# A hybrid decoder layer on one core: 26 of 96 input projections in a stage of their own, 22 of them in pairs with seven block products

## The chip, the core and the metric

The kernel runs on one core of one Trainium2 chip. A core has a matrix engine (PE, TensorE), which reads its two operands from the on-chip memory SBUF and writes to the accumulators in PSUM; three engines for elementwise work (DVE or VectorE, ACT or ScalarE, POOL or GpSimd); and DMA queues, which here are all issued by SP (SyncE), in order. Each engine works through its own list of instructions in a fixed order and waits on semaphores where it needs what another engine makes. The metric is device microseconds of one execution; lower is better.

## The reference, cut to what matters

One layer of a decoder, for a prompt of 1024 tokens and for eight samples of 8 tokens, with the same weights. The kernel treats them as one matrix of TT = 1088 tokens, with the channels on the partitions.

```
h = rmsnorm(x) * (1 + scale) + shift             # scale, shift, gate from a conditioning vector
q, k, v, g_att, z, xBC, dt, g_a, g_b = split(h @ w_in)
att  = 3 groups of dilated windowed attention (prompt; sample over a cache), combined by softmax weights
xBC  = silu(causal_conv4(xBC)); dt = softplus(dt + bias)
y    = chunked_scan(x, dt, B, C, state) + d_skip * x        # Mamba-2 (SSD), chunks of 128
y    = group_rmsnorm(y * silu(z))
out  = sigmoid(g_a) * ((att * silu(g_att)) @ w_att) + sigmoid(g_b) * (y @ w_ssm)
return rmsnorm(x + gate * (out @ w_out)), new caches, new states
```

All sizes are float32, D = 1024. The columns of w_in make 96 tiles of 128 columns (and a narrow one for dt): 12 each of q, k and v (three groups by four pairs of heads), 4 of the attention gate, 16 of z, 24 of x, B and C, 16 of the merge gates.

## The kernel before

Each matrix product of float32 numbers is made of three products of rounded numbers: a value is split into a high part, rounded to the format the matrix engine takes (`fp32r`), and the remainder, and hi x hi, lo x hi and hi x lo are added up in PSUM (`mm3`, lines 193 to 198). So one of the 96 projections is 8 (tiles along the inner dimension) x 3 (terms) x 3 (chunks of 368, 368 and 352 tokens) = 72 matmuls, each with its own load of a 128x128 weight tile. The tiles `h_hi`, `h_lo` of the modulated input stay in SBUF; a weight tile is loaded (`load_w`, `wraw`), split by ACT (`whi`) and DVE (`wlo`), and fetched one projection ahead (`fetch`).

The program has a front (rmsnorm and modulation, with two projections run "early", k by k, as the input tiles come), an attention stage, an SSD stage and an output stage. In the two stages in the middle the order of PE is written out by a recording layer. `run` (line 259) goes through a list of projections, `jobs`. Beside it runs a generator, the side work: `attention` or `side`, which yields how long (in the layer's own count of time) the next step should wait, or after which projection it may come. Every few matmuls of a projection the layer asks whether the side step is due (`Order.poll`) and if so puts the step's matmuls in between. A job that needs a side step to be done first (its marks, for a buffer) makes the layer write out side steps until it is, due or not (`Order.until`). So the order is fixed when the program is built: how much projection work lies between two side steps is what covers the time that DVE, ACT, POOL and DMA need between them.

Side work of the attention stage, for each pair of heads: three prompt groups (scores `s`, softmax on DVE and ACT, transposes `pt`, values `o`), and then the sample block: scores against the cached keys (`sA`, `sB`, with four key tiles `kt` at a time, and `sC`), the softmax of `sm`, its transposes `spt`, the products `so` with seven cached value tiles `vt`, and `soT` to turn the result. `kt`, `vt` and the combination weights `wb` share five buffers (tag `kv`).

Side work of the SSD stage, in four quarters: B and C of a quarter are turned and multiplied (`tt`, `cb`), and then four x tiles, each with `tt` (turn x), `stt` (chunk states), `yo` (carried state), `sts` (state of the samples) and `yd` (diagonal part, with the decay table `csb`). The table is loaded per tile (line 973) into one buffer, which `yd` reads last; DVE subtracts, ACT takes the exponential, DVE multiplies (lines 977 to 985). `sts` and `yd` use two PSUM banks in turn (`bankA`), and DVE frees them (lines 1072 and 1089). At the quarter's end `ms` sums squares by 18 one-column matmuls.

Of the kernel before, what the change touches and what calls it, by code (L numbers as in the profile page):

```python
# [9 lines left out]
F32 = mybir.dt.float32  # L10
# [20 lines left out]
CHUNKS = ((0, 368), (368, 368), (736, 352))  # L31
EPS = 1e-6
# [24 lines left out]
class Order:  # L57
# [47 lines left out]
    def finish(self):  # L105
        self.until(None)
# [3 lines left out]
def trunk(ctx: ExitStack, tc: tile.TileContext, I, O):  # L110
# [64 lines left out]
    wp = hctx.enter_context(pool("wp", 2, side="right"))  # L175
# [49 lines left out]
    def passes():  # L225

        for ks in (range(i, i + 2) for i in range(0, KO, 2)):
            for k in ks:
                yield k, 0, 0
                yield k, 1, 0  # L230
            for k in ks:
                yield k, 0, 1

    def project_early(js, banks):

        ws = [load_w(w_in(j), KO, 128, wp)[:2] for j in js]
        ps = [[b[i](f"early{n}") for i in range(3)] for n, b in enumerate(banks)]
        for k, a, b in passes():
            for w, p in zip(ws, ps):
                for (c0, cn), q in zip(CHUNKS, p):  # L240
                    PE.matmul(q[:, :cn], w[a][:, k, :], (h_hi, h_lo)[b][k][:, c0:c0 + cn], start=(k, a, b) == (0, 0, 0),
                              stop=(k, a, b) == (KO - 1, 0, 1))
# [44 lines left out]
    def w_in(j):  # L287
        return I["w_in"][j]


    with pool("ph0", 2) as p0:
        xT = [p0.tile([128, TT], F32, name=f"xT{k}", bufs=1) for k in range(KO)]
# [13 lines left out]
        def ada(q):  # L306
# [13 lines left out]
            fs = slice(2 * q, 2 * q + 2)  # L320
# [49 lines left out]
        for q in range(4):  # L370
            ada(q)
            for f in (2 * q, 2 * q + 1):
                modulate(f)
        project_early((J_K, J_Q), ([bankPJ] * 3, [bankA, bankA, bankC]))


# [73 lines left out]
    gates = list(range(16))  # L450
# [36 lines left out]
    region = ctx.enter_context(ExitStack())  # L487
    region.enter_context(tc.manual_schedule(engines={mybir.EngineType.PE}))
    with ExitStack() as actx:
# [31 lines left out]
        def attention_jobs(hp, g):  # L521
# [8 lines left out]
            def masks():  # L530
# [3 lines left out]

            yield (("k", n), J_K + g * 4 + hp, (("s", n - 2),) if n > 1 else (),
                   tile_of("k", 2, lambda t, c0, cn, ps: evac_to(t, g, c0, cn, ps)),
                   lambda: store_kv(0, g, hp, tiles[n, "k"]))
            yield (("q", n), J_Q + g * 4 + hp, (("s", n - 2),) if n > 1 else (),
                   tile_of("q", 2, lambda t, c0, cn, ps: evac_to(t, g, c0, cn, ps, 0.125)), masks)
# [287 lines left out]
    with ExitStack() as bctx:  # L827
# [17 lines left out]
        def conv_job(name, j, marks, late, dst):  # L845
# [52 lines left out]
        def jobs():  # L898
            for gr in range(4):
# [389 lines left out]
def _arrays(i):  # L1289
# [18 lines left out]
    for n in ("dt_bias", "a_log"):  # L1308
# [8 lines left out]
        "w_ada": w_ada[:, :2 * D].reshape(8, 128, 2, 4, 256).transpose(3, 0, 1, 2, 4).reshape(4, 8, 128, 512), "w_gate": w_ada[:, 2 * D:].reshape(8, 128, D), "b_gate": i["b_ada"][0][2 * D:],  # L1317
# [52 lines left out]
```

## Time and profile before

| | |
|---|---|
| median of 3 runs | 1938.38 us (1936.6 to 1940.47) |
| profiled execution, its own time | 1937.77 us |
| its span, first to last instruction | 1935.9 us |
| PE busy | 1873.6 us (97%), 13065 matmuls |
| PE weight loads busy | 1760.3 us (91%) |
| DVE / ACT / POOL busy | 1062.1 / 644.9 / 327.7 us |
| DMA | 269.54 MB, mean 139 GB/s |
| granted PE clock, mean | 0.993 |

How to read it: matmuls are pipelined, and a row's duration is that of one matmul from start to modelled end, so durations overlap; what one costs in a stream is the distance between starts. A float32 matmul that isn't split is two records. The "idle" behind a row is the time before it in which the engine had nothing to run, with what ended it. Front to about 69 us, attention to 777, SSD to 1545, then the output stage.

### The profile page before, as it was taken

Reading aid. Unit: us, or ns where it says so; the run is one execution under the profiler, and the core shown is the slowest. Engines: PE = TensorE matmul, PEld = TensorE weight load, DVE = VectorE, ACT = ScalarE, POOL = GpSimd, SP = SyncE. Lnnn points to the kernel's source line nnn. Section 1 sums busy time; section 2 is a strip of 40 time slices with the busy share of each in tenths; the row PEclk is TensorE's granted clock in tenths of the full one; section 3 lists DMA queues with packets and bytes.
Section 4 is the critical chain, followed back from the end, with each engine's and each line's share of the span. In section 5 each row is a group of like instructions: output and inputs, shape, how many; then the busy total and the mean of one; then the engine's idle time right before and its main releaser. Section 6 shows DMA issues by size and latency. Waiting matters only on the chain.

```text
span 1935.9 us, 31991 instructions
## 1 busy us (share of the span) xinstructions
PE 1873.6 (97%) x13065; PEld 1760.3 (91%) x13065; DVE 1062.1 (55%) x1974; ACT 644.9 (33%) x1260; POOL 327.7 (17%) x356
## 2 busy tenths in 40 slices
PE   5999999999999999999999999999999999999998
PEld 4989989988998998999999999999999899999987
DVE  5643243324324323577757775767679655466654
ACT  4443324313423432424342335233533331131222
POOL 2200010001002001132314221422142300000400
PEclk9999999999999999999999999999999999999999
DMA  8322462273256227434443543344233453364322
GB/s 338 121 69 102 132 223 69 87 221 132 96 156 195 83 89 238 148 124 164 148 136 114 169 159 124 117 155 138 81 99 121 153 188 117 127 200 148 123 87 76
DMA packets 108986, 269.54 MB, mean 139 GB/s; under 512 B 41600, under 2 KB 50632, under 8 KB 105576
## 3 DMA queue, kind: packets, MB, share of 16 engines
q1 hardware_dynamic: 108840, 267.51, 42.1%
q8 instruction: 102, 1.67, 0.4%
q14 instruction: 44, 0.36, 0.1%
HBM read 224.93 MB, written 80.26 MB: 158 GB/s over the span
## 4 chain that ended last, share of the span: by engine, by line
PE 50%; DVE 7%; DMA 6%; issue 3%; ACT 2%; POOL 0%; SPq 0%; ACTq 0%; DVEq 0%; POOLq 0%
PE pj L196 12%; PE pj L197 12%; PE pj L198 12%; DMA csb<-cs_d 3%; PE yd L205 2%; PE fo L1207 2%; PE fo L1205 2%; PE fo L1206 2%; PE yo L205 1%; DMA yx<-u_d 1%; DVE wlo L190 1%; DVE csb L977 1%; DVE csb L985 1%; PE sts L205 1%; PE stt L205 1%
## 5 line engine op out<-in xcount | busy, mean ns | idle before, releaser
L196 PE MATMUL pj<-h_hi,whi 128*128 128x368 f32 x2256 | 757.1, 336 | 5.2 <-DVE zs L892 4.7
L198 PE MATMUL pj<-h_lo,whi 128*128 128x368 f32 x2256 | 740.6, 328 | 0.0
L197 PE MATMUL pj<-h_hi,wlo 128*128 128x368 f32 x2256 | 740.1, 328 | 0.0
L196 PEld LDWEIGHTS pj<-h_hi,whi 128*128 128x128 f32 x2256 | 426.1, 189 | 30.9 <-issue 21.1
L197 PEld LDWEIGHTS pj<-h_hi,wlo 128*128 128x128 f32 x2256 | 426.3, 189 | 0.7
L198 PEld LDWEIGHTS pj<-h_lo,whi 128*128 128x128 f32 x2256 | 425.9, 189 | 0.0
L190 DVE TENSOR_TENSOR wlo<-wraw,whi 128x1024 fp32r<-128x1024 f32 (+1 forms) x136 | 163.5, 1202 | 247.8 <-ACT whi L189 245.5
L189 ACT ACTIVATE whi<-wraw 128x1024 fp32r<-128x1024 f32 (+1 forms) x136 | 126.6, 931 | 377.3 <-PE pj L198 369.9
L196 PE MATMUL pj<-yhi,whi 128*128 128x368 f32 (+1 forms) x480 | 157.5, 328 | 1.2 <-DVE acc L1169 1.1
L197 PE MATMUL pj<-yhi,wlo 128*128 128x368 f32 (+1 forms) x480 | 157.7, 328 | 0.2
L198 PE MATMUL pj<-ylo,whi 128*128 128x368 f32 (+1 forms) x480 | 157.1, 327 | 0.0
L626 ACT ACTIVATE pr<-pr,st 128x128 f32<-128x128 f32 (+1 forms) x192 | 83.9, 438 | 88.9 <-DVE st L623 88.7
L197 PEld LDWEIGHTS pj<-yhi,wlo 128*128 128x128 f32 x480 | 90.1, 188 | 3.0 <-issue 2.1
L196 PEld LDWEIGHTS pj<-yhi,whi 128*128 128x128 f32 x480 | 90.1, 188 | 3.0 <-ACT whi L189 1.4
L198 PEld LDWEIGHTS pj<-ylo,whi 128*128 128x128 f32 x480 | 90.1, 188 | 0.0
L875 DVE SCALAR_TENSOR_TENSOR xc<-raw,cw,xc 128x1112 f32<-128x1112 f32 x60 | 82.2, 1369 | 3.1 <-ACT xc L873 2.2
L645 DVE COPY pT<-pt 128x512 f32<-128x512 f32 x40 | 27.6, 689 | 102.3 <-ACT pT L647 40.4
L977 DVE TENSOR_TENSOR csb<-tok,csb 128x2048 f32<-128x2048 f32 x16 | 45.2, 2824 | 45.9 <-DMA csb<-cs_d 45.9
L1174 POOL TENSOR_TENSOR acc<-acc,ta 128x368 f32<-128x368 f32 (+1 forms) x24 | 24.2, 1010 | 263.8 <-DVE ta L1173 263.8
L506 DVE COPY k<-pj 128x368 f32<-128x368 f32 (+2 forms) x44 | 24.0, 581 | 81.3 <-PE pj L198 79.8
L858 ACT ACTIVATE raw<-pj 128x368 f32<-128x368 f32 (+1 forms) x72 | 31.9, 446 | 87.2 <-PE pj L198 84.5
L623 DVE CUSTOM_DVE_ANT_0 pr<-s,msk 128x128 f32<-128x128 f32 (+1 forms) x192 | 55.4, 346 | 7.8 <-PE s L205 7.5
(282 smaller groups left out, 2533.5 us busy)
## 6 DMA issues: line engine op xcount, KB each, us to landing
wraw<-in_w_in SPq DMA_DIRECT2D x96, 512.0 KB, 3.9
csb<-cs_d SPq DMA_DIRECT2D x16, 1088.0 KB, 6.5
kt<-in_kc SPq DMA_DIRECT2D x32, 448.0 KB, 4.6
out_kc<-in_kc SPq DMA_DIRECT2D x32, 448.0 KB, 4.7
out_vc<-in_vc SPq DMA_DIRECT2D x28, 512.0 KB, 5.1
vt<-in_vc SPq DMA_DIRECT2D x28, 512.0 KB, 5.9
sg_d<-sg SPq DMA_DIRECT2D x16, 544.0 KB, 3.0
ecs<-cs_d SPq DMA_DIRECT2D x32, 272.0 KB, 5.0
```

The lines of the kernel that those rows point to most:

```text
L189: S.activation(hi, raw, AF.Copy)
L190: V.tensor_sub(lo, raw, hi.bitcast(F32))
L196: PE.matmul(ps, whi[:, k, :], xhi[k], start=first and k == 0, stop=False)
L197: PE.matmul(ps, wlo[:, k, :], xhi[k], start=False, stop=False)
L198: PE.matmul(ps, whi[:, k, :], xlo[k], start=False, stop=last and k == n - 1)
L205: PE.matmul(out, w, x, **kw)
L623: V.tensor_tensor_reduce(out=pr[:, h, c0:c0 + m], in0=ps[h][:, c0:c0 + m], in1=msk[:, h, w - m:w], scale=-1.0, scalar=3e38, op0=OP.add, op ...
L626: S.activation(pr[:, h, c0:c0 + m], pr[:, h, c0:c0 + m], AF.Exp, scale=-1.0, bias=st[:, 0, h, u:u + 1], accum_out=st[:, 1, h, u:u + 1])
L875: V.scalar_tensor_tensor(c, raw[:, t:t + CONV], cw[:, j, t:t + 1], c, op0=OP.mult, op1=OP.add)
L977: V.tensor_tensor(csb[:, :, :T].rearrange("p h (c l) -> p h c l", l=CH), tok[:, :8, 32 + h0:34 + h0].rearrange("p c h -> p h c")[:, :, :, ...
L1205: PE.matmul(ps, hi, whi[:, k, cs], start=k == 0, stop=False)
L1206: PE.matmul(ps, lo, whi[:, k, cs], start=False, stop=False)
```

## The change

A stage of its own stands between the front and the attention stage. It makes 26 projections: all 12 of q, the 8 even ones of z, and 6 of the 16 merge gates. Two of the gates are the early ones now (k and q were before), and two more are made whole, as before, at the two ends of the stage (`whole`). The other 22 go in 11 pairs. For a pair, the two 128-column weight tiles and the input are taken as 2x2 blocks (output tile by inner half; inner half by half of the tokens), and Strassen's scheme in Winograd's form makes the four result blocks from seven block products instead of eight. Each product has 4 inner tiles x 3 terms, for two halves of 272 columns: 7 x 2 x 12 = 168 matmuls of 272 columns, where two plain projections have 144 of 368 and 352. The combinations of input blocks (T1 to T4) are made once, the weight combinations (`factors`) for every pair, one pair ahead. Results go to DRAM (`q_d`, `z_d`, `sg_d`) and q and z are read back when the stages need them; the lists of jobs of the two stages lose these projections. The side work and its waits (the yields) are unchanged. In the front, `modulate` takes an input tile with its partner four tiles on, and keeps the modulated input in float32 for the combinations.

```diff
+    def project_early(js, banks, pool_, raws):
 ...
-            fs = slice(2 * q, 2 * q + 2)
+            fs = slice(q, KO, KH)
 ...
-            S.activation(h_hi[f][:, :T], h[:, :T], AF.Identity, bias=shift)
-            S.activation(h_hi[f][:, T:], h[:, T:], AF.Copy)
-            V.scalar_tensor_tensor(h_lo[f][:, :T], h[:, :T], shift, h_hi[f][:, :T].bitcast(F32), op0=OP.add, op1=OP.subtract)
-            G.tensor_tensor(h_lo[f][:, T:], h[:, T:], h_hi[f][:, T:].bitcast(F32), op=OP.subtract)
+            S.activation(h[:, :T], h[:, :T], AF.Identity, bias=shift)
+            S.activation(h_hi[f], h, AF.Copy)
+            V.tensor_sub(h_lo[f], h, h_hi[f].bitcast(F32))
 ...
-        project_early((J_K, J_Q), ([bankPJ] * 3, [bankA, bankA, bankC]))
+        project_early((J_GA, J_GA + 1), ([bankPJ] * 3, [bankA, bankA, bankC]), we, rawp)
 ...
+    for k in (0, 3, 1, 2):
+        n = k + KH
+        b11, b12, b21, b22 = xT[k][:, L], xT[k][:, R], xT[n][:, L], xT[n][:, R]
+        t = [tp.tile([128, 2, TH], F32R, name=f"t{k}{i}") for i in range(4)]
+        V.tensor_sub(b11, b12, b11)
+        G.tensor_tensor(b12, b22, b12, op=OP.subtract)
+        V.tensor_sub(b22, b22, b11)
+        V.tensor_sub(b21, b21, b22)
+        for x, r in zip(t, (b11, b22, b12, b21)):
+            S.activation(x[:, 0], r, AF.Copy)
+            V.tensor_sub(x[:, 1], r, x[:, 0].bitcast(F32))
 ...
+    whole(2, [(hi[:, k, :], lo[:, k, :]) for k in range(KO)], bankPJ, we.tile([128, TT], F32, tag="y", name="sg", bufs=1))
 ...
+        def factors(j0, j1):
+            (a11, a12), (a21, a22) = load_raw(j0), load_raw(j1)
 ...
+            G.tensor_tensor(s1, a21, a22, op=OP.add)
+            def parts(src):
+                op = ring.tile([128, 2, KH, 128], F32R, tag="op", name="op")
+                S.activation(op[:, 0], src, AF.Copy)
+                V.tensor_sub(op[:, 1], src, op[:, 0].bitcast(F32))
+                return op
+            yield parts(a11)
+            V.tensor_sub(s2, s1, a11)
+            yield parts(s2)
 ...
+        def product(ps, op, b, c0, cn, first=True):
+            cs = slice(c0, c0 + cn)
+            for k in range(KH):
+                hi, lo = H[k][b]
+                PE.matmul(ps, op[:, 0, k, :], hi[:, cs], start=first and k == 0, stop=False, skip_group_check=not first)
+                PE.matmul(ps, op[:, 1, k, :], hi[:, cs], start=False, stop=False, skip_group_check=not first)
+                PE.matmul(ps, op[:, 0, k, :], lo[:, cs], start=False, stop=k == KH - 1, skip_group_check=not first)
+        work = ([("q", n) for n in range(12)] + [("z", n) for n in apart["z"]] + [("gate", 3), ("gate", 4)])
 ...
+            for half in range(2):
 ...
+                product(pa, ops[0], B11, c0, cn)
+                S.activation(u1, pa, AF.Copy, scale=scale)
+                step()
+                product(pc, ops[1], T2, c0, cn)
+                V.scalar_tensor_tensor(u2, pc, scale, u1, op0=OP.mult, op1=OP.add)
+                step()
 ...
+        fetch(J_K)
+        whole(5, ws, bankPJ, rows.tile([128, TT], F32, tag="y", name="sg"))
+    rctx.close()
+    cut_psum("att", p=3, a=2, b=2, c=1)
 ...
-    gates = list(range(16))
+    gates = list(range(6, 16))
 ...
+            def queries():
+                t = tiles[n, "q"] = ap_.tile([128, TT], F32, tag="q", name="q", bufs=2)
+                SP.dma_start(out=t, in_=q_d[n])
 ...
-            yield (("q", n), J_Q + g * 4 + hp, (("s", n - 2),) if n > 1 else (),
-                   tile_of("q", 2, lambda t, c0, cn, ps: evac_to(t, g, c0, cn, ps, 0.125)), masks)
 ...
+                if name[0] == "x" and name[1] in apart["z"]:
+                    zs = tiles["z", name[1]] = bp.tile([128, TT], F32, tag="zs", name="zs", bufs=2)
+                    SP.dma_start(out=zs, in_=z_d[name[1]])
 ...
-                    yield z_job(xt, (("x", xt - 2),) if xt > 1 else ())
-                    if xt % 2 and xt < 13:
-                        yield from gate_jobs(1)
+                    if xt not in apart["z"]:
+                        yield z_job(xt, (("x", xt - 2),) if xt > 1 else ())
```

`step()` makes the next factor of the next pair in a pair's second half. Five gates still come at the end of the attention stage and five at the end of the SSD stage.

## Rows read from the trace of the kernel before

**Rows 1.** The page, part 1: busy time, share and instructions of each engine.
```profile
PE 1873.6 (97%) x13065; PEld 1760.3 (91%) x13065; DVE 1062.1 (55%) x1974; ACT 644.9 (33%) x1260; POOL 327.7 (17%) x356
```
**Rows 2.** The page, part 4: the chain that ended last, by engine.
```profile
PE 50%; DVE 7%; DMA 6%; issue 3%; ACT 2%; POOL 0%; SPq 0%; ACTq 0%; DVEq 0%; POOLq 0%
```
**Rows 3.** Windows, one SSD quarter: PE, PEld, DVE, ACT, POOL busy, clock, DMA.
```profile
1170.00:1361.00 191.00, 185.54 (x1287) 178.32 (x1286) 134.05 (x210) 69.17 (x105) 56.55 (x49) 0.99 0.40 132
```
**Rows 4.** Timeline of PE (start, duration): two runs of matmuls, first and last.
```profile
76.72 0.33 PE L196 MATMUL pj<-h_hi,whi 128*128 128x368 f32 x1
...
80.72 0.33 PE L196 MATMUL pj<-h_hi,whi 128*128 128x368 f32 x1
...
1916.66 0.28 PE L1205 MATMUL fo<-wohi,yhi 128*64 128x256 f32 x1
...
1925.71 0.28 PE L1206 MATMUL fo<-wohi,ylo 128*64 128x256 f32 x1
```
**Rows 5.** Timeline of the weight loads, SSD stage.
```profile
1479.62 1.86 PEld L205 LDWEIGHTS stt<-xde,Bk 128*128 128x128 f32 x16 [1.12 <-POOL xde L1008]
```
**Rows 6.** Waits: us in total, times, longest.
```profile
PEld pj L196 <- issue: 22.3, 83, 0.4
```
**Rows 7.** The tile of the time-step weights: ns min/median/max, starts, forms; landing.
```profile
L393 ACT ACTIVATE dtw<-dtw x1: 402/402/402, 63.5 to 63.5; 128x256 fp32r<-128x256 f32 x1
L394 DVE TENSOR_TENSOR dtw<-dtw,dtw x1: 415/415/415, 65.0 to 65.0; 128x256 fp32r<-128x256 f32 x1
...
DMA to landing us min/median/max: 2.2/2.2/2.2
```
**Rows 8.** Timeline of PE, the first sample block.
```profile
237.17 0.88 PE L205 MATMUL sC<-ks,QF 128*128 128x64 f32 x6
247.30 0.93 PE L209 MATMUL spt<-pack,sm 128*128 128x128 f32 x7
...
252.51 1.56 PE L789 MATMUL so<-vs,spN 64*128 64x256 f32 x6
254.70 2.39 PE L205 MATMUL so<-vt,spT 128*32 128x128 f32 x80
```
**Rows 9.** Timelines of DVE, ACT and SP's queue, the same block.
```profile
240.34 0.79 DVE L769 TENSOR_SCALAR sm<-sm,smn 128x1088 f32<-128x1088 f32 x1
...
249.61 0.49 ACT L784 ACTIVATE spN<-spt 64x384 f32<-64x384 f32 x1 [0.23 <-PE spt L209]
...
228.78 1.96 SPq L752 DMA_DIRECT2D kt<-in_kc  x3
...
255.41 1.78 SPq L794 DMA_DIRECT2D vt<-in_vc  x2
```
**Rows 10.** The tiles kt (first) and vt (second): from issue to landing.
```profile
DMA to landing us min/median/max: 3.1/4.6/5.8
...
DMA to landing us min/median/max: 3.8/5.9/7.8
```
**Rows 11.** Timeline of PE after the one-column matmuls at a quarter's end.
```profile
1361.03 2.44 PE L165 MATMUL ms<-onesc,sq 128*128 128x1 f32 x18 [0.99 <-POOL sq L1097]
1363.40 0.67 PE L196 MATMUL pj<-h_hi,whi 128*128 128x368 f32 x1
...
1369.39 0.37 PE L197 MATMUL pj<-h_hi,wlo 128*128 128x368 f32 x1
```
**Rows 12.** Windows, the same place (columns as in rows 3).
```profile
1365.00:1370.00 5.00, 5.00 (x19) 5.00 (x19) 4.92 (x6) 4.98 (x5) 0.00 (x0) 0.55 0.37 110
```
**Rows 13.** Timeline of DVE, the second x tile of a quarter.
```profile
1241.97 0.22 DVE L1089 TENSOR_TENSOR u<-u,yd 128x64 f32<-128x64 f32 x1
...
1250.29 3.33 DVE L977 TENSOR_TENSOR csb<-tok,csb 128x2048 f32<-128x2048 f32 x1 [2.43 <-DMA csb<-cs_d]
...
1267.32 0.67 DVE L1072 TENSOR_TENSOR sst<-sst,sts 128x512 f32<-128x512 f32 x1
```
**Rows 14.** Windows, that tile from yd to yd (columns as in rows 3).
```profile
1241.95:1275.45 33.50, 31.74 (x230) 29.68 (x230) 23.38 (x39) 9.89 (x15) 8.80 (x4) 1.00 0.48 174
```
**Rows 15.** The page, part 5: the convolution's multiply-adds.
```profile
L875 DVE SCALAR_TENSOR_TENSOR xc<-raw,cw,xc 128x1112 f32<-128x1112 f32 x60 | 82.2, 1369 | 3.1 <-ACT xc L873 2.2
```

More of the change, by code (lines that the diff above doesn't have):

```diff
@@ L31 @@
 CHUNKS = ((0, 368), (368, 368), (736, 352))
+KH = KO // 2
+TH = TT // 2
 EPS = 1e-6
@@ L223, in copy_some, with block @@
         del copies[:n]
[L225 to L236, printed above, removed]
-        ps = [[b[i](f"early{n}") for i in range(3)] for n, b in enumerate(banks)]
[L238 to L242, printed above, removed]
+    def project_early(js, banks, pool_, raws):
+        ws = [load_w(w_in(j), KO, 128, pool_, raws=raws)[:2] for j in js]
+        ps = [[b[i](f"early{n}") for i in range(3)] for n, b in enumerate(banks)]
+        def block(w, p, k, a, b):
+            for (c0, cn), q in zip(CHUNKS, p):
+                PE.matmul(q[:, :cn], w[a][:, k, :], (h_hi, h_lo)[b][k][:, c0:c0 + cn], start=(k, a, b) == (0, 0, 0),
+                          stop=(k, a, b) == (KO - 1, 0, 1))
+        for q in range(KH):
+            parts = [(k, a, 0) for k in (q, q + KH) for a in range(2)] + [(k, 0, 1) for k in (q, q + KH)]
+            if q < KH - 1:
+                for part in parts:
+                    for w, p in zip(ws, ps):
+                        block(w, p, *part)
+            else:
+                for w, p in zip(ws, ps):
+                    for part in parts:
+                        block(w, p, *part)
         for j, p in zip(js, ps):
@@ L288, in w_in @@
         return I["w_in"][j]
-    with pool("ph0", 2) as p0:
-        xT = [p0.tile([128, TT], F32, name=f"xT{k}", bufs=1) for k in range(KO)]
+    rctx = ExitStack()
+    rawp = rctx.enter_context(pool("raw", 2))
+    fctx = ExitStack()
+    xp = fctx.enter_context(pool("xT", 1))
+    xT = [xp.tile([128, TT], F32, name=f"xT{k}", bufs=1) for k in range(KO)]
+    we = fctx.enter_context(pool("we", 2))
+    with pool("ph0", 2, side="right") as p0:
         cT = p0.tile([128, 8, 9], F32, name="cT", bufs=1)
@@ new lines, in trunk, with finish @@
+    T1, T2, T3, T4, B11, B21, B22 = range(7)
+    q_d = dram.tile([12, 128, TT], F32, name="q_d")
+    z_d = dram.tile([NX, 128, TT], F32, name="z_d")
+    apart = {"z": range(0, NX, 2), "gate": range(6)}
+    def finish(kind, n, y, spare):
+        if kind == "gate":
+            S.activation(y, y, AF.Tanh, scale=0.5)
+            SP.dma_start(out=sg_d[n], in_=y)
+        elif kind == "z":
+            th = spare("th")
+            S.activation(th, y, AF.Tanh, scale=0.5)
+            V.scalar_tensor_tensor(y, th, 1.0, y, op0=OP.add, op1=OP.mult)
+            SP.dma_start(out=z_d[n], in_=y)
+        else:
+            SP.dma_start(out=q_d[n], in_=y)
@@ new lines, in column, with pieces @@
+    def column(kind, n):
+        return {"gate": J_GA + n, "z": J_Z + n, "q": J_Q + n % 3 * 4 + n // 3}[kind]
+    def pieces(kind, n, y, c0, cn):
+        if kind != "q":
+            return [(y[:, c0:c0 + cn], lambda ap: ap)]
+        d = DIL[n % 3]
+        m = max(0, min(c0 + cn, T) - c0)
+        out = [(y[:, :T].rearrange("p (r i) -> p i r", r=d)[:, c0 // d:(c0 + m) // d, :],
+                lambda ap: ap[:, :m].rearrange("p (i r) -> p i r", r=d))] if m else []
+        if m < cn:
+            out.append((y[:, c0 + m:c0 + cn], lambda ap: ap[:, m:]))
+        return out
@@ new lines, in trunk, with whole @@
+    for n in range(2):
+        y = we.tile([128, TT], F32, tag="y", name="sg", bufs=1)
+        for (c0, cn), q in zip(CHUNKS, early.pop(J_GA + n)):
+            S.activation(y[:, c0:c0 + cn], q[:, :cn], AF.Tanh, scale=0.5)
+        SP.dma_start(out=sg_d[n], in_=y)
+    def whole(n, ws, banks, y):
+        for c0, cn in CHUNKS:
+            ps = banks("pj")[:, :cn]
+            for k in range(KO):
+                hi, lo = ws[k]
+                PE.matmul(ps, hi, h_hi[k][:, c0:c0 + cn], start=k == 0, stop=False)
+                PE.matmul(ps, lo, h_hi[k][:, c0:c0 + cn], start=False, stop=False)
+                PE.matmul(ps, hi, h_lo[k][:, c0:c0 + cn], start=False, stop=k == KO - 1)
+            S.activation(y[:, c0:c0 + cn], ps, AF.Tanh, scale=0.5)
+        SP.dma_start(out=sg_d[n], in_=y)
```

99 lines of the change are left out of this document (90 added, 9 removed).

## The prediction

> **What bounds the kernel now.** I read the page first: TensorE is busy 97% of the span and VectorE 55% [rows 1], so a microsecond of matmul taken out should be a microsecond of time, as long as no other chain takes its place. The chain of waits says the same with a reservation: TensorE holds half of it, and VectorE, DMA and "issue" hold most of the rest [rows 2]. That rest is in two places. In the attention stage the sample half is one long dependent chain per head pair. In the SSD stage a quarter lasts about 191 us, in which TensorE works 185.5 and VectorE 134 [rows 3]; TensorE is the bound there, but not by far. What hides both chains today is projection matmuls, which the recording layer puts between their steps. So the change has to be read twice: what 22 cheaper projections save, and what happens to the steps whose cover is taken away.
>
> **The stage itself.** A plain projection is 72 matmuls. In a run of the 368-column ones, the 24th after the first starts 4.00 us later, 0.1667 us each; the 256-column ones of the final projection start 9.05 us apart over 76 steps, 0.119 each [rows 4]. On the line between them 352 columns cost 0.160 and 272 cost 0.126. A pair of plain projections is 2 x (48 x 0.1667 + 24 x 0.160) = 23.7 us. A Strassen pair is seven products of two halves of 12 matmuls, 168 matmuls of 272 columns: 21.2 us. It saves 2.5 us, and eleven pairs 27.6 us. The unknown is whether narrower matmuls keep that pace, since each has a weight load of its own. The nearest row is favourable: 16 loads of full 128x128 weights in 1.86 us, one every 0.11 us [rows 5], are quicker than 0.126. From below, the 256-column rows (0.119) make it 40 us; from above, if a 272-column matmul cost what a 368-column one does, 1848 matmuls would be 75 us dearer and the stage would lose 48. I take 0.126, since the 256-column row is only 16 columns away. The Trainium skill (TensorE: Matmul & The Clock Gate, Back-to-back issue gap) gives a matmul N / 2.4 GHz plus 2.5 ns; the rows show 13 ns over N / 2.4 at 368 columns and 12 at 256. By that rule a pair would save about 2.7 us and the stage 29; the rows decide, and the 24 extra matmuls of a pair carry the difference.
>
> VectorE and ScalarE make seven factors of half a weight tile per pair where they made two whole ones. I put nothing on this: both are free half of the time and more [rows 1], and the factors of a pair are made one pair ahead, behind the products of the second half of the pair before, each needed 10 us after its buffer is free. If that cover fails, a pair waits for its factors at its start.
>
> **Fewer returns to the projections.** When TensorE comes back from a side step to a projection it loses 0.27 us 83 times, 22.3 us in all [rows 6]. The recorded order has 184 stretches of projections now and 149 after: 35 fewer, and 83 in 184 of them cost something, so 4 us less. Bounds 0 and 9.
>
> **Start and end of the stage.** The front makes one more pass on ScalarE for each of eight tiles, and the T matrices have to be ready when the second product starts; one whole projection lies between. I put 3 us on it (0 to 15: nothing like it is in the trace). At the end the time-step weights are loaded behind a store that waits for the last gate projection, since SP's queue keeps its order; today they are there long before. Landing 2.2, conversion 0.40 and 0.42 [rows 7], and about 1.5 for the evacuation and the issues ahead of them (an estimate without a row): 4.5 us in which TensorE, in its fixed order, has nothing else. Sum 7.5.
>
> **The sample block.** This is the first place where cover goes. Here is TensorE's order around the softmax of the second head pair (sC are its last scores, spt the transposes of the probabilities, so the products with the cached values); before, 57 projection matmuls stand between sC and spt, and 18 more ahead of so:
> ```order
> L196 MATMUL pj<-h_hi_90,whi 128x368
> L197 MATMUL pj<-h_hi_90,wlo 128x368
> L198 MATMUL pj<-h_lo_98,whi 128x368
> L209 MATMUL spt<-pack,sm 128x128 x7
> L209 MATMUL spt<-pack,sm 64x128 x3
> L196 MATMUL pj<-h_hi_91,whi 128x368
> L197 MATMUL pj<-h_hi_91,wlo 128x368
> ```
> and in the changed kernel the same place reads:
> ```order
> L209 MATMUL sA<-kt,QZ 32x512 x4
> L209 MATMUL sB<-kt,QZ 32x128 x4
> L209 MATMUL sB<-kt,QZ 32x256 x4
> L209 MATMUL sC<-ks,QF 128x64 x3
> L213 MATMUL spt<-pack,sm 128x128 x7
> L213 MATMUL spt<-pack,sm 64x128 x3
> L989 MATMUL so<-vs,spN 128x256 x3
> L209 MATMUL so<-vt,spT 32x128 x56
> L213 MATMUL soT<-pack,so 128x128 x2
> L213 MATMUL vt<-pack,vT 128x128 x8
> ```
> All cover is gone, and this holds for three of the four head pairs; only the last keeps gates between its steps. The waits, from the first head pair of today. From the start of sC (237.17) to the scaled probabilities (240.34 + 0.79) it is 4.0 us, of which sC itself takes 0.9: 3.1 us of wait [rows 8, 9]. The transposes last from 247.30 until their last copy at 250.10, 2.8 us with some 1.4 of matmul in it: 1.4. Two of the seven value tiles can only be requested when the first ones have been read: 0.7 us into so, 1.8 us of issue for both, then 5.9 us to land (3.8 at best), while only 2.4 us of matmuls stand ahead [rows 8 to 10]: 3 to 5 us. With the copy ahead of soT that is 8 to 10 us a block. I take 8, as a part is waited for today already: 24 us. In two of the blocks the second set of keys also has 12 matmuls of cover (51 today) against 1.3 + 4.6 us of issue and landing [rows 9, 10]: 3.9 each, 7.8. And TensorE slows after a thin stretch: after 18 one-column matmuls and 1 us of idling the granted clock from 1365 to 1370 is 0.55, that is mostly the lower of its two levels (1.2 instead of 2.4 GHz), and 19 matmuls take 5.99 us instead of 3.17 [rows 11, 12]: 2.8 us, three times, 8.4. Sum 40 (18 to 50). The Trainium skill warns of this (TensorE: Matmul & The Clock Gate, HAM oscillation): gaps without matmuls bring TensorE back to the half clock, and each new burst starts cold. Today's block, interleaved with projections, shows no such fall.
>
> **The x tiles of the SSD stage.** With 8 of the 16 z projections and six gates moved away, a quarter keeps 8 projections where it had 10 and up to two gates, and the recorded order thins most at the third tile of a quarter. Here it is in the second quarter, from the last projection matmuls ahead of yo (products with the carried state) on; sts is the state update and yd the diagonal part. Before:
> ```order
> L196 MATMUL pj<-h_hi_95,whi 128x368
> L197 MATMUL pj<-h_hi_95,wlo 128x368
> L198 MATMUL pj<-h_lo_103,whi 128x368
> L205 MATMUL yo<-CT,sta 128x128 x7
> L209 MATMUL yoT<-pack,ys 128x128 x2
> L205 MATMUL sts<-xdm_10279,Bs 128x512
> L205 MATMUL sts<-xdm_10280,Bs 128x512
> L205 MATMUL sts<-xdm_10279,Bs 128x512
> L205 MATMUL sts<-xdm_10280,Bs 128x512
> L196 MATMUL pj<-h_hi_96,whi 128x368
> L197 MATMUL pj<-h_hi_96,wlo 128x368
> ```
> and after:
> ```order
> L202 MATMUL pj<-h_lo_102,whi 128x352
> L209 MATMUL yo<-CT,sta 128x128 x7
> L213 MATMUL yoT<-pack,ys 128x128 x2
> L209 MATMUL sts<-xdm_11848,Bs 128x512
> L209 MATMUL sts<-xdm_11849,Bs 128x512
> L209 MATMUL sts<-xdm_11848,Bs 128x512
> L209 MATMUL sts<-xdm_11849,Bs 128x512
> L209 MATMUL yd<-csb,xdt 64x128 x16
> L209 MATMUL yd<-csb,xdt 64x64 x2
> L200 MATMUL pj<-h_hi_87,whi 128x368
> ```
> The 30 matmuls between sts and yd are gone, and from the yd before to this one only 39 + 33 = 72 are left (132 in the tile measured below). What TensorE waits for there is VectorE's list of a tile. Today, in a second tile of a quarter, it runs from the last yd addition (1241.97) over the decay table (1250.29, after 2.4 us of waiting for its DMA, whose single buffer is free only when yd is done) to the second state addition (1267.99): 26 us [rows 13]. yd needs that addition's PSUM bank back. TensorE's own part of that tile is 31.7 us with 132 projection matmuls (21.7 us), so 10 us without them [rows 14]. With 72 it has 21.8 us of work. VectorE's list now also holds the convolution of a later tile, 3 x 1.37 us and more [rows 15], of which I let half fall into its gaps: 28.5 us, and yd 2.2 after it, 30.7. So the third tile waits 9 us. The second tile keeps 102 matmuls (26.8 us of work) and waits 2 us more than today. With 1 us at the turn of the quarter that is 12 us a quarter; the first has 12 matmuls less (14), the last keeps its cover from gates (3): about 40. From below, if VectorE's gaps take all of the convolution and nothing else shifts: 12. From above, if nothing fits and each second and third tile is late by the whole of it: 75.
>
> **Sum.** The profiled execution took 1937.8 us (the median of the runs is 1938.4, so it stands for them). 1937.8 - 27.6 - 4 + 7.5 + 40 + 40 = 1994 us.
>
> **Rivals.** *The cover was surplus.* VectorE is idle 45% of the time and could run ahead, so that the x tiles wait no longer than today, and the value tiles land under other work (4 us a block instead of 8). Then 1937.8 - 27.6 - 4 + 7.5 + 12 + 7.8 = 1933, faster. It decides from the point where all new waits stay under 24 us. For it: the list's idle stretches [rows 13]. Against it: the three blocks have nothing between their steps, and 13 us of them is plain latency. 10%.
> *The clock falls at the x tiles too.* The third tile's waits and the second's, seven in all, each bring the half clock for some 6 us: 7 x 2.8 = 20 more, 2014. For it: the fall in [rows 11, 12] came after little more than such a gap. Against it: matmuls stand on both sides, and the second tile's waits are short. The rule of the skill quoted above would have it so. 20%.
> *The stage doesn't do what it says*, because a 272-column matmul costs like a 368-column one: 75 more, 2069. [rows 5] speak against it. 4%.
>
> **How the numbers follow.** My own case has 65%, and its own range is 1965 to 2018. For 8 in 10 the range takes in part of the surplus rival and of the clock rival: 1950 to 2034. This kernel's measurement tells some 0.2% (4 us) from no change. Faster than that: 10%, nearly all of it the surplus rival; within it 2%; slower 88%.
>
> **What would show it.** Right: the new stage's matmuls start every 0.126 us with TensorE at 100%; in the chain, DVE, ACT and DMA at sm, spt and vt in three blocks of the attention stage, with gaps of 3 to 5 us; TensorE's idle time before yo, sts and yd at the third x tile. Wrong: TensorE still at 97% after the stage, or matmuls of 0.13 us and more inside it, or a wait of more than a few microseconds at the stage's two ends.

## The result and the profile after

The changed kernel takes 2076.98 us (median of 4 runs, 2073.17 to 2082.17) against 1938.8 for the kernel before in the same session: a ratio of 1.0715, 95% interval 1.0685 to 1.0746. Slower was right; 1994 us was too low by 83, and 2034, the upper end of the range, by 43. The profiled execution has a span of 2080.2 us, 144.3 more than before; it is the slowest of the four, 5 us above their median, so differences between traces come out some us larger than those between medians.

The page of the changed kernel, parts 1, 2 (one row) and 4, answers to [rows 1, 2]:
```profile
PE 1919.9 (92%) x13329; PEld 1778.4 (85%) x13329; DVE 1194.0 (57%) x2158; ACT 682.6 (33%) x1330; POOL 389.6 (19%) x402
...
PEclk9999999999899899899999899899899899999999
...
PE 66%; DVE 13%; DMA 10%; ACT 4%; issue 4%; POOL 2%; SPq 1%; DVEq 0%; ACTq 0%; POOLq 0%
```
TensorE was to do less and is busy 46 us longer, in a span in which its share falls from 97 to 92%. Two things must have happened: it waits more, and it takes longer for its matmuls. A window for each stage parts them. The stages are cut at TensorE's own marks: the first time-step matmul (dt), the last soT, the last sum of squares (ms) of the SSD stage. Columns as in [rows 3]: span, busy time (instructions) of PE, PEld, DVE, ACT, POOL, granted clock, DMA. The kernel before:
```profile
68.80:769.90 701.10, 691.57 (x5173) 633.20 (x5173) 248.05 (x707) 241.99 (x648) 51.95 (x92) 1.00 0.42 133
769.90:1544.50 774.60, 755.70 (x5249) 728.87 (x5248) 552.49 (x843) 281.81 (x423) 230.86 (x201) 0.99 0.41 134
1544.50:1935.90 391.40, 382.38 (x2207) 358.12 (x2206) 223.54 (x364) 93.93 (x150) 24.23 (x24) 1.00 0.41 136
```
The changed kernel, the same three stages:
```profile
343.50:999.70 656.20, 616.57 (x4512) 544.58 (x4513) 235.97 (x697) 209.09 (x591) 37.25 (x90) 0.95 0.44 139
999.70:1698.50 698.80, 628.16 (x4253) 587.83 (x4253) 549.81 (x805) 245.93 (x367) 247.84 (x202) 0.93 0.40 130
1698.50:2080.20 381.70, 373.27 (x2134) 349.03 (x2134) 221.59 (x363) 91.78 (x146) 24.26 (x24) 0.99 0.42 138
```
Each matmul that is gone should give 0.1645 us back (a plain projection of 72 takes 11.85). In the attention stage 661 are gone, 108.7 us, and the stage is only 44.9 shorter: 63.8 us are lost. Of these 30.1 are idle time (span minus PE went from 9.5 to 39.6), and 33.7 are PE being busy longer than its remaining matmuls need. The same sum for every stage (us):

| stage | work taken out or in | stage changed by | lost | idle time | busy too long | forecast of the loss |
|---|---|---|---|---|---|---|
| to the first dt | +256.9 | +274.7 | 17.8 | | | 7.5 |
| attention | -108.7 | -44.9 | 63.8 | +30.1 | +33.7 | } 76, of it 8.4 |
| SSD | -163.8 | -75.8 | 88.0 | +51.7 | +36.3 | } at the half clock |
| output | -12.0 | -9.7 | 2.3 | -0.6 | +2.9 | 0 |
| sum | -27.6 | +144.3 | 171.9 | | | 83.5 |

The work of the front is eleven pairs at 21.2 us and the two plain gate projections. The granted clock beside these stages (0.95 and 0.93, before 1.00 and 0.99) says where "busy too long" comes from. Here is the first sample block on TensorE, which answers to [rows 8]:
```profile
512.41 0.88 PE L209 MATMUL sC<-ks,QF 128*128 128x64 f32 x6
517.21 2.65 PE L213 MATMUL spt<-pack,sm 128*128 128x128 f32 x10 [3.92 <-DVE sm L969]
520.43 2.92 PE L989 MATMUL so<-vs,spN 64*128 64x256 f32 x6 [0.57 <-ACT spN L984]
523.28 4.12 PE L209 MATMUL so<-vt,spT 128*32 128x128 f32 x80
529.93 0.78 PE L209 MATMUL so<-vt,spT 128*32 128x128 f32 x16 [2.52 <-DMA vt<-in_vc]
532.48 1.08 PE L209 MATMUL so<-vt,spT 128*32 128x128 f32 x16 [1.78 <-DMA vt<-in_vc]
534.18 0.69 PE L213 MATMUL soT<-pack,so 128*128 128x128 f32 x2 [0.62 <-DVE so L1004]
...
539.75 0.51 PE L200 MATMUL pj<-h_hi,whi 128*128 128x368 f32 x1
540.06 0.51 PE L201 MATMUL pj<-h_hi,wlo 128*128 128x368 f32 x1
```
The waits are those of the forecast: 3.9 us for the probabilities, 2.5 and 1.8 for the last two value tiles, 0.6 ahead of soT; 9.4 us with the small ones, where 8 was taken. But the 80 products that took 2.39 us now take 4.12, and the projection matmuls at the end start every 0.31 us instead of 0.1667. The windows of the same place (columns as above) show the clock:
```profile
510.00:515.00 5.00, 3.29 (x32) 1.70 (x30) 3.55 (x9) 1.22 (x2) 2.92 (x9) 1.00 0.76 217
515.00:520.00 5.00, 2.60 (x10) 1.71 (x10) 3.01 (x15) 2.57 (x6) 0.00 (x0) 0.66 1.04 422
520.00:525.00 5.00, 4.57 (x40) 3.41 (x44) 0.00 (x0) 0.38 (x1) 0.00 (x0) 0.50 0.70 232
525.00:530.00 5.00, 2.48 (x57) 2.07 (x52) 0.00 (x0) 0.00 (x0) 0.00 (x0) 0.81 0.93 280
530.00:535.00 5.00, 2.61 (x36) 1.72 (x37) 0.52 (x2) 0.00 (x0) 0.00 (x0) 0.53 1.05 239
535.00:540.00 5.00, 4.88 (x21) 3.47 (x20) 3.30 (x8) 0.00 (x0) 3.03 (x2) 0.50 0.92 277
540.00:545.00 5.00, 5.00 (x30) 5.00 (x30) 5.00 (x7) 0.77 (x3) 2.71 (x1) 0.95 0.07 18
```
0.50 is the lower of the two levels, 1.2 GHz. It holds from about 517 to 540, for most of the block. In between the full clock comes back once, at the end of the 80 products (0.81 from 525 to 530); TensorE spends most of that time waiting for a value tile, and the clock falls again in the next products. The forecast had priced the fall at 2.8 us for each block, behind it, and at nothing inside. By the Trainium skill's rule (TensorE: Matmul & The Clock Gate, HAM oscillation) each burst behind a gap starts cold. The windows agree for the transposes at 517.21 and what follows them (0.50), but not for the 16 products at 529.93, which start at the full clock behind a wait of 2.52 us (1.00 from 529 to 530, 0.65 from 530 to 531). The forecast had quoted the rule and applied it to one gap a block.

In the SSD stage the third x tile of the second quarter reads, on TensorE (the first row is from the tile before it):
```profile
1282.71 2.23 PE L209 MATMUL yd<-csb,xdt 128*64 128x128 f32 x36
...
1300.32 0.38 PE L209 MATMUL yo<-CT,sta 128*128 128x128 f32 x2
1303.99 1.95 PE L209 MATMUL yo<-CT,sta 128*128 128x128 f32 x8 [3.29 <-DVE sta L1235]
1306.93 0.80 PE L209 MATMUL yo<-CT,sta 128*128 128x128 f32 x2 [0.98 <-DVE sta L1235]
1309.03 0.80 PE L209 MATMUL yo<-CT,sta 128*128 128x128 f32 x2 [1.30 <-DVE sta L1235]
...
1312.84 1.22 PE L209 MATMUL sts<-xdm,Bs 128*128 128x512 f32 x2 [1.73 <-DVE sta L1235]
1314.23 4.24 PE L209 MATMUL yd<-csb,xdt 128*64 128x128 f32 x36 [0.17 <-DVE sst L1274]
```
and on VectorE, which has no gap here:
```profile
1293.45 4.59 DVE L1179 TENSOR_TENSOR csb<-tok,csb 128x2048 f32<-128x2048 f32 x1
...
1299.86 3.04 DVE L1078 SCALAR_TENSOR_TENSOR xc<-raw,cw,xc 128x1112 f32<-128x1112 f32 x1
...
1303.48 1.80 DVE L1235 SCALAR_TENSOR_TENSOR sta<-sta,eall,stt 128x64 f32<-128x64 f32 x9
1305.21 1.48 DVE L1187 TENSOR_TENSOR csb<-csb,CB 128x1088 f32<-128x1088 f32 x1
1306.60 0.46 DVE L1235 SCALAR_TENSOR_TENSOR sta<-sta,eall,stt 128x64 f32<-128x64 f32 x2
...
1307.12 1.21 DVE L1085 SCALAR_TENSOR_TENSOR xc<-raw,xc 128x1024 f32<-128x1024 f32 x1
1308.70 0.46 DVE L1235 SCALAR_TENSOR_TENSOR sta<-sta,eall,stt 128x64 f32<-128x64 f32 x2
```
TensorE waits 7.3 us, where 9 was the forecast; the state steps (sta) that it needs stand between pieces of the convolution (xc) and of the decay table (csb). Then the clock: yd's 36 matmuls take 4.24 us, in the tile before 2.23, and the window of the waits has 0.50:
```profile
1310.00:1315.00 5.00, 3.10 (x14) 1.65 (x14) 5.00 (x11) 0.00 (x0) 0.00 (x0) 0.50 0.47 168
```
Over the SSD stage the waits of TensorE (us, times, longest) are, in the kernel before:
```profile
PE yo L205 <- DVE sta L1033: 3.0, 4, 1.1
```
and in the changed kernel:
```profile
PE yo L209 <- DVE sta L1235: 42.2, 31, 3.3
PE sts L209 <- DVE sta L1235: 5.2, 4, 1.7
```

How much of "busy too long" is the clock can be estimated from the same trace: in windows of half a microsecond, TensorE's busy time times the missing share of the clock adds up to 28.7 us in the attention stage (0.0 before) and 37.5 in the SSD stage (8.5 before). So the half clock makes about 58 of the 70 us; the other 12 were not traced.

The new stage itself did what was forecast: its matmuls start from 92.8 to 325.8, 233.0 us for 1848, 0.126 each.

### The profile page after: what moved, and what is told of

It reads as the page before. It is cut to its first block, busy times and chain, and to the rows that moved or that the text cites. A ratio compares the mean times of both kernels' runs of the same rounds, so it can differ in the third digit from the quotient of the medians.

```text
span 2080.2 us, 33110 instructions
## 1 busy us (share of the span) xinstructions
PE 1919.9 (92%) x13329; PEld 1778.4 (85%) x13329; DVE 1194.0 (57%) x2158; ACT 682.6 (33%) x1330; POOL 389.6 (19%) x402
## 4 chain that ended last, share of the span: by engine, by line
PE 66%; DVE 13%; DMA 10%; ACT 4%; issue 4%; POOL 2%; SPq 1%; DVEq 0%; ACTq 0%; POOLq 0%
PE pj L200 13%; PE pj L201 12%; PE pj L202 12%; DMA csb<-cs_d 5%; PE pw L505 4%; PE pw L506 4%; PE pw L507 4%; DVE xc L1078 2%; PE s L209 2%; PE pt L213 2%; PE o L209 2%; PE fo L1409 2%; PE fo L1408 2%; PE fo L1407 2%; DVE csb L1187 1%
## 5 line engine op out<-in xcount | busy, mean ns | idle before, releaser
L200 PE MATMUL pj<-h_hi,whi 128*128 128x368 f32 (+1 forms) x1680 | 570.1, 339 | 6.8 <-ACT raw L1058 3.9
L201 PE MATMUL pj<-h_hi,wlo 128*128 128x368 f32 (+1 forms) x1680 | 555.8, 331 | 0.0
L202 PE MATMUL pj<-h_lo,whi 128*128 128x368 f32 (+1 forms) x1680 | 555.3, 331 | 0.0
L200 PEld LDWEIGHTS pj<-h_hi,whi 128*128 128x128 f32 x1680 | 321.8, 192 | 29.2 <-issue 18.5
L201 PEld LDWEIGHTS pj<-h_hi,wlo 128*128 128x128 f32 x1680 | 321.8, 192 | 0.8
L202 PEld LDWEIGHTS pj<-h_lo,whi 128*128 128x128 f32 x1680 | 320.9, 191 | 0.0
L194 DVE TENSOR_TENSOR wlo<-wraw,whi 128x1024 fp32r<-128x1024 f32 (+1 forms) x113 | 128.4, 1137 | 95.8 <-ACT whi L193 92.5
L1078 DVE SCALAR_TENSOR_TENSOR xc<-raw,cw,xc 128x1112 f32<-128x1112 f32 x60 | 105.8, 1763 | 10.8 <-ACT xc L1076 10.7
L505 PE MATMUL pw<-t,op 128*128 128x272 f32 x352 | 101.7, 289 | 1.0 <-ACT op L486 1.0
L506 PE MATMUL pw<-t,op 128*128 128x272 f32 x352 | 101.1, 287 | 0.3 <-DVE op L487 0.3
L507 PE MATMUL pw<-t,op 128*128 128x272 f32 x352 | 101.0, 287 | 0.0
L845 DVE COPY pT<-pt 128x512 f32<-128x512 f32 x40 | 27.6, 691 | 127.7 <-PE pt L213 76.6
L209 PE MATMUL yo<-CT,sta 128*128 128x128 f32 x224 | 50.1, 348 | 44.7 <-DVE sta L1235 42.2
L209 PEld LDWEIGHTS yo<-CT,sta 128*128 128x128 f32 x224 | 37.3, 220 | 56.6 <-DVE sta L1235 51.2
```

The source lines that it names most:

```text
L200: PE.matmul(ps, whi[:, k, :], xhi[k], start=first and k == 0, stop=False)
L201: PE.matmul(ps, wlo[:, k, :], xhi[k], start=False, stop=False)
L202: PE.matmul(ps, whi[:, k, :], xlo[k], start=False, stop=last and k == n - 1)
L209: PE.matmul(out, w, x, **kw)
L505: PE.matmul(ps, op[:, 0, k, :], hi[:, cs], start=first and k == 0, stop=False, skip_group_check=not first)
L506: PE.matmul(ps, op[:, 1, k, :], hi[:, cs], start=False, stop=False, skip_group_check=not first)
```

## The experiments

Theory: the 22 projections were cover; without them the chains of the two stages show as waits, and each wait brings the half clock on top. Rivals: the stage itself disturbs the rest; VectorE's list alone is the bound; it is the order of VectorE's and SP's queues.

**Which stage loses for which projections.** e1 moves only the queries into pairs (and makes four plain gates ahead of the attention stage), e2 only z and two gates.
```diff
-work = ([("q", n) for n in range(12)] + [("z", n) for n in apart["z"]] + [("gate", 3), ("gate", 4)])
+work = [("q", n) for n in range(12)]                                        # e1
+work = [("z", n) for n in apart["z"]] + [("gate", 3), ("gate", 4)]          # e2
 ...                                  # the stages' lists of jobs get the others back
```


> Only the 12 query projections (6 pairs) go through the new stage; the 8 z projections and the gates stay in the SSD stage as before. My theory (each removed projection was cover for a chain of waits in its own stage): the attention stage still loses about 64 us against its matmuls, the SSD stage loses nothing and lasts 775 us as before; 1937.8 - 15 (6 pairs) + 18 (front and ends as measured) + 64 = 2005 us. Rival (the stage itself disturbs the rest of the kernel by its memory traffic and buffers): the SSD stage still loses some 88 us, about 2090. Rival (the losses of the two stages are one and the same shortage, shifted): between, 2040 and more.

> Only the 8 z projections and two gates (5 pairs) go through the new stage; the 12 query projections stay in the attention stage. My theory: the attention stage lasts 701 us as before, the SSD stage loses 88 us against its matmuls; 1937.8 - 12.5 + 18 + 88 = 2031 us. Rival (the stage itself disturbs): attention loses some 64 us too, about 2095.

Measured: e1 2036.86 us (ratio 1.049, 1.0449 to 1.0532), e2 2021.84 (1.042, 1.0383 to 1.0457). In e1 the attention stage lasts 655.0 us (656.2 in the changed kernel, with as many matmuls). In e2 it lasts 729.6, which is 701.1 before and 143 more matmuls (23.5), 5 over: the stage in front doesn't disturb it. The SSD stage lasts 693.8 in e2 (698.8 in the changed kernel) and 773.8 in e1 (774.6 before). But e1 has 128 matmuls less there than the kernel before (21.1 us), so it loses 20 us, where the rival said 88; some 17 of them are in the first and the last quarter, which hold fewer matmuls. So each stage loses, in the main, for its own projections.

e1 came out 32 us above its sum, which had left out its gates: with four of them in front, one instead of five ends the SSD stage. The SSD stage lost the 20 us above, and the output stage became 24.9 us shorter where 220 matmuls, 36.2 us, had gone.

**The products' saving.** e3 does the 22 as plain projections in the same stage.
```diff
-product(pa, ops[0], B11, c0, cn)     # ... seven products a half
+for x in work: plain(*x, ws)         # 72 matmuls of 368 and 352 columns each
```


> The same 22 projections in the same stage, but each as 72 plain matmuls and without the block products (the T matrices are made and not used). My theory (the products save what was forecast): the stage lasts 22 x 11.85 = 261 us instead of 233, the rest as in the changed kernel, 2077 + 27.6 = 2105 us. Rival (VectorE's and ScalarE's extra work for the factors is what costs): 2077 or less.

Measured 2104.02 us (1.0853, 1.0807 to 1.0899): 27.0 above the changed kernel, 27.6 forecast; in the trace the time-step matmuls start 28.9 us later. The saving is real and about as large as reckoned; making the factors costs nothing that shows.

e3 also shows how much a stage varies. Its SSD stage is the same code as the changed kernel's and lasts 686.5 us, 12.3 less, of which 6.5 are PE's busy time; the same attention code lasts 653.0 to 658.7 in the changed kernel, e1, e3, e9 and e12. So a few microseconds in one trace's SSD stage prove nothing. Reckoned from e3's trace, the SSD stage loses 76 us and not 88, and the half clock makes 51 us and not 58.

**The clock.** e5 puts matmuls that nothing uses into the waits (three blocks, second and third x tiles), 280 in all.
```diff
+def fill(n):
+    ps = bankPJ("fill")
+    for i in range(n):
+        PE.matmul(ps[:, :368], h_hi[i % KO][:, 0:128], h_hi[i % KO][:, :368], start=i == 0, stop=i == n - 1)
...
+            fill(20 if hp < 3 else 0)        # behind sC; others ahead of vt, yo and sts
```


> The changed kernel with matmuls that nothing uses (368 columns, into a spare PSUM tile) in the places where TensorE waits: 20 behind sC and 8 ahead of each of the last two value tiles in the first three sample blocks; 9 and 4 ahead of the two yo groups of each second x tile of a quarter, 18 and 4 of each third, 4 ahead of its two sts. They are about as long as the waits there. Theory (part of the loss is the half clock that follows a wait): the waits stay as long, the matmuls behind them come back to the full clock, and some 6 us a block and 6 us a quarter come back: 2077 - 42 = 2035 us. Rival (the loss is waiting alone): 2077 or a little more, since the extra matmuls only take the place of waits.

Measured 2050.85 us (1.0569, 1.0524 to 1.0614), 26 less than the changed kernel with 280 matmuls more. The block that took 4.12 us for its 80 products:
```profile
513.51 3.58 PE L217 MATMUL fill<-h_hi 128*128 128x368 f32 x20
517.63 0.98 PE L220 MATMUL spt<-pack,sm 128*128 128x128 f32 x7 [0.53 <-DVE sm L977]
...
521.55 2.39 PE L209 MATMUL so<-vt,spT 128*32 128x128 f32 x80
```
and the two stages (columns as above):
```profile
343.40:986.30 642.90, 613.73 (x4620) 547.26 (x4621) 235.62 (x697) 208.88 (x591) 37.55 (x90) 0.99 0.44 142
986.30:1667.70 681.40, 632.98 (x4425) 600.68 (x4424) 549.33 (x805) 246.32 (x367) 252.52 (x202) 0.98 0.41 134
```
The clock is back at 0.99 and 0.98. Without the 108 and 172 fills (0.1667 each, 18.0 and 28.7 us) PE is busy 595.7 and 604.3 us, so "busy too long" shrinks from 33.7 to 12.8 and from 36.3 to 12.4: 45 us come back with the clock (37 against e3's trace). The fills cost 46.7 us and replaced only 32.7 of idle time, so 14 of the 45 are paid away again, and the two stages are 31 us shorter. This is the fastest execution of e5 against the slowest of the changed kernel; between medians the whole gain is 26, not the 42 of the expectation.

**VectorE's list.** e6 and its control e7 leave out two of three multiply-adds of every convolution.
```diff
-for t in range(1, 4):
+for t in range(1, 2):
     V.scalar_tensor_tensor(c, raw[:, t:t + CONV], cw[:, j, t:t + 1], c, op0=OP.mult, op1=OP.add)
```


> The changed kernel with two of the three multiply-adds of each convolution left out (48 VectorE instructions of 1.4 to 1.7 us, some 19 us a quarter). Theory (in the x tiles TensorE waits for VectorE's list, which holds the convolution of a later tile between the steps that yo, sts and yd need): the SSD stage, 699 us, gets 5 to 10 us a quarter shorter, 2077 - 30 = 2047 us. Rival (the wait is the latency of the dependent chain, whatever VectorE does beside it): under 2 us a quarter, 2070 to 2077.

> The kernel before with the same two of three multiply-adds left out, as the control of the run above: both theories expect no change where TensorE is the bound, 1938 us within 5; if it gets faster by as much as the changed kernel does, VectorE's list was a cost all along and says nothing on the change.

Measured: e6 2041.12 us (1.0519, 1.0473 to 1.0564), 36 less than the changed kernel; e7 1932.91 (0.9971, 0.9949 to 0.9993), 6 to 8 less than before. Waits and SSD stage of e6:
```profile
PE yo L209 <- DVE sta L1235: 25.5, 23, 1.8
```
```profile
998.00:1652.70 654.70, 611.83 (x4253) 578.89 (x4253) 476.78 (x757) 246.56 (x367) 251.57 (x202) 0.96 0.42 139
```
73 us less VectorE work shortens the stage by 44.1 us, 4.1 in the control (770.5 from 774.6). So some 40 of the SSD stage's 88 lost microseconds hang on VectorE's list, or 28 of 76 if e3's trace is the base. Of the 44.1, 27.8 are TensorE's idle time and 16.3 its busy time, with the clock up from 0.93 to 0.96.

e9 and e10 take 4.7 us of VectorE's work from each tile without leaving anything out: the subtraction of the decay table goes to ScalarE.
```diff
-V.tensor_tensor(csb[:, :, :T]..., tok..., csb[:, :, :T]..., op=OP.subtract)
-    S.activation(m, m, AF.Relu)
+    for c in range(9):
+        S.activation(e, e, AF.Relu, scale=-1.0, bias=tok[:, c, 32 + h0 + h:33 + h0 + h])
```


> The changed kernel with the subtraction of the decay table (L1179 and L1182, 3.6 and 1.1 us of VectorE for each x tile) folded into ScalarE's Relu, as 18 activations with a bias for each tile; nothing is left out of the result. Theory (VectorE's list is what the x tiles wait for): 4.7 us of 34 us of list per tile go, of which about half come back, 16 x 2.4 = 38 us, 2077 - 38 = 2039 us. Rival (the chain's latency, not the list: the table is now made by a longer chain on ScalarE): 2077 or a little more.

> The kernel before with the same edit. Theory (TensorE bounds its SSD stage, with 19 us of idling in 775): a gain of up to what the convolution cut brought there, 1940.9 - 8 = 1933 us, which would be the fastest version that computes everything. Rival (ScalarE's 5 us in place of 2 make something else late): 1941 or more.

Measured: e9 2070.04 us (1.0663, 1.0639 to 1.0688), 7 less than the changed kernel, with intervals that just meet; e10 1955.75 (1.0079, 1.0058 to 1.0099), slower than before. The rivals were nearer. VectorE lost 61 us of work in e9's SSD stage and the stage 8.4, which is no more than it varies by. In e10 a wait has grown that is 2.7 us in the kernel before:
```profile
PE tt L209 <- DVE xc L882: 22.4, 4, 7.2
```
The convolution starts and ends on ScalarE, and its list grew by 51 us: 288 short activations are 85.1 us of busy time where 32 long ones were 33.8. That they stand ahead of the convolution is read from this wait and was not tried by itself. If it is so, what counts is which instruction stands ahead of the one that is waited for, and not the engine's load. It also leaves open how much of e6's gain is VectorE's time and how much is the shorter chain of the convolution itself, which e6 cuts too.

**Order.** e8 makes the combination on GpSimd and loads the time-step weights before the last gate of the new stage.
```diff
-V.tensor_add(at[:, :T], at[:, :T], wb)
+G.tensor_tensor(at[:, :T], at[:, :T], wb, op=OP.add)
...
+wr = wp.tile([128, KO, 128], F32, tag="wraw", name="dtw", bufs=3)[:, :, :32]   # ahead of load_raw(J_GA + 5)
```


> The changed kernel with two orders mended: the combination of the three groups' outputs (L932 to L938) is made on GpSimd instead of VectorE, so that VectorE's queue doesn't wait for it ahead of the next group's softmax; and the time-step weights are loaded and split before the last gate projection of the new stage. Theory (these are the part of the misses that is order, not cover): 5 us at the time-step projection and 3 us in each of three blocks, 2077 - 14 = 2063 us. Rival (the chain of the block is just as long without them): only the 5 us, 2072 us.

Measured 2071.01 us (1.0676, 1.0631 to 1.0721): the intervals overlap, so the time alone doesn't tell it from no change. The trace does: dt starts at 337.7 instead of 343.5, and attention lasts 648.0, under the 653.0 to 658.7 of the runs with the old order; the SSD stage lasts 4.4 longer, which is within what it varies by.

**Where cover stands.** e4 moves four tail gates, e12 sends the odd z projections to the front.
```diff
+yield from gate_jobs((2, 0, 0, 5)[hp])               # e4, behind the head pair's gate
+if i == 2 and gr < 2: yield from gate_jobs(1)        # e4, SSD stage
-apart = {"z": range(0, NX, 2), "gate": range(6)}
+apart = {"z": range(1, NX, 2), "gate": range(6)}     # e12
```


> The changed kernel with the same matmuls; four of the five gate projections at the end of the SSD stage are moved: two behind the first head pair's gate (so that matmuls stand between the steps of the first sample block again), one each behind the third x tile of the first and second quarter. My theory (lost cover): the first sample block gives back about 20 us and the two third tiles 13 us each, the last x tile loses 10 for want of the gates; 2077 - 36 = 2041 us. Rival (VectorE's list is the bound in the x tiles, whatever TensorE does meanwhile): only the block, 2057 to 2067 us. Rival (the clock falls for another reason): 2077.

> The changed kernel with the odd z projections in the new stage instead of the even ones, so that the third tile of a quarter keeps its projection and the second and fourth lose theirs. Forecast's reading (the third tile is where it is thin): its waits of some 9 us a quarter shrink by more than the other tiles grow, 2077 - 20 = 2057 us. Rival (a quarter is short of cover as a whole, wherever the hole is): 2077 within 10.

Both missed. e4 took 2092.6 us (1.0782, 1.0744 to 1.0821), slower than the changed kernel or level with it. The first block gave 12.3 us back (attention 11.6 longer with 145 matmuls, 23.9 us, more), not 20. The two SSD quarters with a gate got 11.3 and 4.2 longer for 11.85 of matmuls each, so 8 us came back, not 26. What had been taken from the end was paid there: the last quarter became 9.9 us shorter where 22.9 of matmuls had gone, and the output stage 10.7 for 24.2, so some 26 were lost. e12 took 2114.03 (1.089, 1.0868 to 1.0912): the SSD stage lasts 735.9 us, 37 more, 9.9 of them for 60 more matmuls, with new waits for ScalarE's first state step (15.9 us) and GpSimd's xde (13.7). So taking z from the second and fourth tiles costs more than taking it from the first and third. Where the projections stand matters, by a rule that neither theory had, and which stays open.

**Together.** e11 is e5, e8 and e9 in one.


> The changed kernel with the unused matmuls in the waits, the combination on GpSimd and the early time-step weights, and the decay table on ScalarE. If the three causes (half clock, VectorE's list, order) are apart, the gains add: 2077 - 26 - 6 - 38 = 2007 us. If the list and the clock are one (a shorter wait leaves no half clock to mend), 2020 us. Below 1941 it would beat the kernel before, which neither theory expects.

Measured 2044.41 us (1.0535, 1.0514 to 1.0556): the gains don't add (6 us on top of e5, whose interval overlaps). No version here that computes the whole result beats the kernel before.

## Why the forecast was wrong

- **The stage: right.** 21.2 us a pair, 27.0 saved (e3) for 27.6. The Trainium skill (TensorE: Matmul & The Clock Gate, Back-to-back issue gap) gives the rule that the prediction quoted for isolated matmuls, not for a stream in which each has its own weight load; here a matmul took 13 ns over N / 2.4, and the sum rightly went by the rows.
- **Start and end of the stage: 17.8 for 7.5.** The wait for the time-step weights was 5.5 us (4.5 forecast); e8 takes it away. The rest is the start, priced at 3 without a row: TensorE waits 5.6 and 3.2 us for the first whole projection's weights, and its first matmuls then start every 0.31 us, at the half clock:
```profile
75.38 0.68 PE L454 MATMUL pj<-h_hi,whi 128*128 128x368 f32 x1 [5.56 <-ACT whi L193]
79.24 0.67 PE L455 MATMUL pj<-h_hi,wlo 128*128 128x368 f32 x1 [3.19 <-DVE wlo L194]
...
80.02 0.51 PE L454 MATMUL pj<-h_hi,whi 128*128 128x368 f32 x1
80.32 0.51 PE L455 MATMUL pj<-h_hi,wlo 128*128 128x368 f32 x1
```
- **The waits: nearly right, in part by luck.** For the sample blocks, the x tiles and the returns 67.8 us of idle time were forecast (24 + 7.8 + 40 - 4); the two stages have 81.8 more than before, 30.1 (31.8 for the blocks) and 51.7 (40). In the attention stage the second keys, 7.8 in the sum, cost 2.1 us, and the prompt groups' softmax (pr), not in it, 4.9 more than before:
```profile
PE pt L213 <- ACT pr L826: 7.4, 6, 1.6
...
PE sA L209 <- DMA kt<-in_kc: 2.1, 5, 0.6
```
against, before:
```profile
PE pt L209 <- ACT pr L626: 2.5, 4, 1.1
```
In the SSD stage the four quarters have 15.1, 14.9, 11.6 and 10.1 us more idle time than before; 14, 12, 12 and 3 were forecast. So most of the excess is the last quarter, whose gates were to keep it covered.
- **The half clock: the step that failed.** 8.4 us were forecast, "three times, 8.4", for one fall behind each block and none at the x tiles. Measured: 70.0 us of PE time beyond what its matmuls need, of which the granted clock accounts for about 58, half of them in each stage (51 in e3's trace); e5 gets 45 of the 70 back with matmuls that compute nothing. So this term is some 50 of the 88 us by which the sum was short of the profiled execution; the start and end are 10, the waits 14, and the untraced busy time most of the rest. The rival *The clock falls at the x tiles too* named the mechanism and gave it 20 us at the x tiles, by seven waits; the trace has 31 waits at yo alone and 29 us. For the attention stage's 29 us the sum had its 8.4: a block is not one gap but four in a row.
- *The cover was surplus* (10%) was wrong: it needed all new waits under 24 us, and they are 81.8. *The stage doesn't do what it says* (4%) was wrong by e3.

## What to carry to other kernels

When work is taken from between the steps of a latency chain, price the new gaps twice: the wait itself, and the matmuls between and behind the waits that then run at half the clock. Here the waits were 82 us and the half clock 51 to 58, about twice what the cheaper algorithm saved. Part a lost stage by windows into idle time and busy time against the matmul count; only the first part is a wait.

## What was not expected of the hardware

280 matmuls of 368 columns that nobody reads made the kernel 26 us faster (e5); the granted clock of the two stages was 0.99 and 0.98 instead of 0.95 and 0.93.

A VectorE instruction's time depended on what GpSimd did beside it. The convolution's multiply-add took 1369 ns in the mean before [rows 15] and 1763 after, with the same shape. Of the 60 after, the 44 that ran with no TENSOR_TENSOR of GpSimd beside them took 1.36 to 1.38 us, as all 60 before; of the 16 that ran beside one, 15 took 2.56 to 3.05, and one that had started ahead of GpSimd's took 1.37. The one at 1299.86 above takes 3.04 while GpSimd scales the state:
```profile
1299.75 1.98 POOL L1266 TENSOR_TENSOR sst<-sst,eall 128x1024 f32<-128x1024 f32 x1
```
The Trainium skill (GPSIMD Engine Reference, 1. Specifications) names contention between GpSimd and VectorE instructions with two SBUF inputs, which this instruction has. The trace agrees; no run here took the GpSimd work away. In sum the 60 lengthened VectorE's list by 24 us; how much of that TensorE waited for was not measured.
